# A decoder block on one core: norm weight spread by transposes into PSUM, the first weight tile in token quarters, the compression's transposes two steps later

## The chip, the cores and the metric

One NeuronCore of a Trainium2 chip. The engines are TensorE (PE, with its weight loads as PEld), VectorE (DVE), ScalarE (ACT), GpSimd (POOL) and SyncE (SP), which here issues nearly all DMAs. Times are microseconds of the device for one execution; a result is the median of several runs.

## The reference, cut to what matters

A pre-norm block over 512 tokens of width 1024, in fp32: an RMSNorm, one wide input projection, two attention mixers (A: an indexer picks the top 128 keys; B: 8 heads in 2 groups with a compressed, a selected and a window branch), a gated merge, and a squared-ReLU MLP.

```
h = rmsnorm(x, norm_mix[l])          # x * rsqrt(mean(x*x) + EPS) * norm_mix
proj = h @ w_in[l]
...
blk = blk.transpose(0, 1, 3, 2, 4).reshape(B, n_c, G, CMP_BLOCK * D)
return jax.nn.gelu(blk @ w1) @ w2    # compress_blocks: keys and values of 31 blocks
...
o = (gb[:, :, 0, :, :, None] * o_c + gb[:, :, 1, :, :, None] * o_s
     + gb[:, :, 2, :, :, None] * o_w)
```

## The kernel before

Products are kept near fp32 by splitting each operand into a high part (fp32r) and a remainder: `mm3` adds high x high, high x low and low x high. The high part is a cast on ScalarE, the low part a subtraction (for weights on GpSimd, for activations mostly on VectorE).

**The start.** The 512 tokens come as four tiles x0 to x3 of 128. For each tile `squares(j)` lets ScalarE square it with a row sum and take the root; `scaled(j, half)` lets VectorE multiply 512 columns by the row factor and by `gmix`, the norm weight on all 128 partitions; `turned(j, half)` transposes four 128x128 blocks on TensorE into a PSUM tile `tr` (two buffers), from which ScalarE writes `hTh` and VectorE `hTl`, the normed activations with features on partitions. Three weight tiles of 128 columns (`wf` 0 to 2, made by `split_first`) then give the products `pks`, `pqb0` and `pkw`: `first_tile(i)` yields them one matmul at a time, 24 per half of the tokens (16 with the high weights, 8 with the low ones), and the program hand-places these steps between the transposes (`first_steps`). The order on TensorE, VectorE and ScalarE in this part mostly follows the written one; each engine executes its list strictly in order. `warm_up(n)` puts n idle matmuls on TensorE. Then come `ptok` (the values of all tokens) and the jobs.

**The middle.** Attention runs as 96 small units; per unit TensorE makes logits, VectorE the biased minimum (`nls`, `nlw`), ScalarE the exponential (`pbs`, `pbw`), TensorE transposes (`ts`, `tw`), VectorE and ScalarE write `PTs`, `PTw`, and `ob` multiplies by the values. Between the steps TensorE does projection matmuls (`pqb`, `pg`) from a queue of jobs, and at two places per unit `hook` advances one step of a list of side jobs: `cmp_keys`, `cmp_values` and, per group, `cmp_probs`. `turned_hidden` transposes the hidden layer of the compression (`zk` to `ztk`, `zv` to `ztv`); it waits until `zk` is in the program and then `YH` further steps. If a head ends before its group's compressed probabilities `PTc` are in the program, its compressed product is put into `late[g]` and made at the end of `cmp_probs` (`oc`). TensorE's order in this part is the written one. On the other engines the framework's scheduler orders the instructions.

`split_both` writes the two head pairs of a group as high and low part (`obh`, `obl`) for the branch-B products, which start after head 7.

Of the kernel before, what the change touches and what calls it, by code (L numbers as in the profile page):

```python
# [38 lines left out]
YV, YK, YT = (2,2,3)  # L39
MB = 2  # L40
LA = 1
YH = 4
SG = ()
NWARM = 12
PITCH = 384
PTW = 1664

# [17 lines left out]
def block_kernel(ctx, tc, x, norm_mix, w_in, pe_k, w1_k, w2_k, pe_v, w1_v, w2_v, rel_bias,  # L65
# [109 lines left out]
        xt.append(t)  # L175

    x_in(0)
    gmix = ep.tile([P, DM], F32, name="gmix")
    gm = rows_of(norm_mix)
    ld(gmix[:, 0:S], gm[:, 0:S])  # L180
    ld(ident, c_id)
    x_in(1)
    ld(gmix[:, S:DM], gm[:, S:DM])
    for a, what in enumerate((C_KS, 2, 3, C_QB, C_KW)):
        if what < NT:
            x_in(what)
        else:
            raws.append(raw_cols([(what, P)], f"wr_f{what}"))
# [20 lines left out]

    def scaled(j, half):  # L210
        cs = slice(half * S, (half + 1) * S)
        V.scalar_tensor_tensor(xs[j][:, cs], xt[j][:, cs], rs[j], gmix[:, cs], op0=ALU.mult, op1=ALU.mult)

    def turned(j, half):

# [7 lines left out]

    wf = []

    def split_first(hi_eng=None):
        wf.append(split_w(raws[len(wf)], [P, KT, P], f"wf{len(wf)}", hi_eng))

    def first_tile(i):
        hi, lo = (lambda y: lambda k: wf[i][y][:, k, :])(0), (lambda y: lambda k: wf[i][y][:, k, :])(1)  # L230
        for half in range(2):
            ts = slice(half * 256, half * 256 + 256)
            yield from mm3_steps(outs[i][:, ts], hi, lo, lambda k: hTh[:, k, ts], lambda k: hTl[:, k, ts], KT)

    W = (1,2,2,2)
    squares(0)()
    scaled(0, 0)
    recip1 = squares(1)
    warm_up(W[0])
    l00 = turned(0, 0)  # L240
    scaled(0, 1)
    recip1()
    scaled(1, 0)
    l00()
    warm_up(W[1])
    l01 = turned(0, 1)
    scaled(1, 1)
    split_first()
    l01()
    warm_up(W[2])  # L250
    l10 = turned(1, 0)
    l10()
    recip2 = squares(2)
    warm_up(W[3])
    l11 = turned(1, 1)
    recip2()
    scaled(2, 0)
    l11()
    outs = [ps("mm", "pks"), ps("mm", "pqb0"), None]
    ft = [first_tile(i) for i in range(3)]  # L260

    def first_steps(i, n):
        for _ in range(n):
            next(ft[i])

    SP = (5, 10, 6, 2)
    scaled(2, 1)
    recip3 = squares(3)
    first_steps(0, SP[0])
    l20 = turned(2, 0)  # L270
    recip3()
    scaled(3, 0)
    l20()
    split_first()
    first_steps(0, SP[1])
    l21 = turned(2, 1)
    scaled(3, 1)
    l21()
    first_steps(0, SP[2])
    l30 = turned(3, 0)  # L280
    l30()
    first_steps(0, 24 - SP[0] - SP[1] - SP[2])
    first_steps(1, SP[3])
    l31 = turned(3, 1)
    l31()
    first_steps(1, 24 - SP[3])
    split_first()
    wt_h = ep.tile([P, KT, 352], F32R, name="wt_h")
    wt_l = ep.tile([P, KT, 352], F32R, name="wt_l")
    for k in range(0, KT, 4):  # L290
        A.copy(wt_h[:, k:k + 4], wt_r[:, k:k + 4])
        G.tensor_sub(wt_l[:, k:k + 4], wt_r[:, k:k + 4], wt_h[:, k:k + 4].bitcast(F32))
    outs[2] = ps("lg", "pkw")
    for i in (2, 0, 1, 2):
        first_steps(i, 24)
    for f in ft:
        for _ in f:
            pass
# [555 lines left out]
    def cmp_probs(g):  # L854

        def run():
            cbias = t2.tile([P, NT, 4, 32], F32, tag="cbias", name=f"cbias{g}")
            bt = t2.tile([P, 512], F32, tag="wk", bufs=3, name=f"bt{g}")
            for r in range(4):
                src = d_fwd[:, 4 * g + r]  # L860
                ld(bt[32 * r:32 * r + 32],
                   bass.AP(tensor=src.tensor, offset=src.offset + 496, ap=[[8 * LF - 16, 32], [1, 512]]))
            yield
            yield
            yield
            t = ps("ov", f"cbt{g}")
            for j in range(NT):
                PE.transpose(t[:, j * P:(j + 1) * P], bt[:, j * P:(j + 1) * P], ident)
            yield
            V.tensor_copy(cbias.rearrange("p j h c -> p (j h c)"), t)  # L870
            ptc = t2.tile([P, 2, S], F32R, tag="ptc", bufs=1, name=f"PTc{g}")
            for j in range(0, NT, 2):
                yield
                lg = ps("ov", f"lc{g}{j}")
                for jj in range(2):
                    for r in range(4):
                        c0 = 256 * jj + 64 * r
# [12 lines left out]
                yield  # L890
                A.activation(L, L, AF.Exp)
                yield
                yield
                s = t2.tile([P, 16], F32, tag="cs", bufs=1, name=f"cs{g}{j}")[:, :8]
                V.reduce_sum(s, L, axis=AX.X)
                V.tensor_scalar(s, s, 1.0e-30, None, op0=ALU.max)
                V.reciprocal(s, s)
                V.tensor_mul(s, s, gcmp[:, g, j:j + 2].rearrange("p j r -> p (j r)"))
                V.tensor_tensor(L, L, s[:, :, None].to_broadcast([P, 8, 32]), op=ALU.mult)
                for _ in range(YT):  # L900
                    yield
                t = ps("ov", f"tc{g}{j}")
                for jj in range(2):
                    PE.transpose(t[:, jj * P:(jj + 1) * P],
                                 L[:, 4 * jj:4 * jj + 4].rearrange("p r c -> p (r c)"), ident)
                yield
                js = slice(j * P, (j + 2) * P)
                A.copy(ptc[:, 0, js], t[:, :2 * P])
                V.tensor_sub(ptc[:, 1, js], t[:, :2 * P], ptc[:, 0, js].bitcast(F32))
            PTc[g] = ptc  # L910
            for f in late[g]:
                yield
                rest = f()
                yield
                if rest:
                    rest()

        return run

    late = [[], []]  # L920


    class Unit:
# [109 lines left out]
    def nsa_end(h, PTw, box):  # L1033
        def last():
            o, g = box[0], h // 4
            direct = PTc[g] is not None
            yield from av_steps(o, PTw(), 3 + g, False, not direct)
            if direct:
                cmp_av(o, h, False)
            assert h != 4 or PTc[0] is not None  # L1040
            if h % 2 == 0:
                ob.append(fp.tile([P, S], F32, tag="opb", bufs=2, name=f"opb{h}"))
            aux.append(lambda: add_o(o, ob[h // 2], h % 2, True))
            if not direct:
                def add(pr=ob[-1]):
                    o = ps("ov", f"oc{h}")
                    cmp_av(o, h, True)
                    return lambda: add_o(o, pr, h % 2, False)

                late[g].append(add)  # L1050
            if h % 2 == 1:
                jobs.insert(0, q_job("a", h // 2))
            if h == 3:
                side.append(cmp_probs(1)())
            if h % 4 == 3:
                def split_pair(pr):
                    oh = t1.tile([P, S], F32R, tag=f"kk{g}", bufs=4, name=f"obh{pr}")
                    ol = t1.tile([P, S], F32R, tag=f"kk{g}", bufs=4, name=f"obl{pr}")
                    A.copy(oh, ob[pr])
                    G.tensor_sub(ol, ob[pr], oh.bitcast(F32))  # L1060
                    obp.append((oh, ol))

                def split_both():
                    aux.extend(lambda pr=pr: split_pair(pr) for pr in (h // 2 - 1, h // 2))

                if direct:
                    split_both()
                else:
                    late[g].append(split_both)
            if h == 7:  # L1070
                cps.close()
                op[0] = pool(os_, "op", "left")
                jobs.extend(branch_b_job(c) for c in range(8))
            yield

        return last
# [529 lines left out]
```

## Time and profile before

| | us |
|---|---|
| median of 3 runs | 791.1 (789.76 to 792.16) |
| the profiled execution, its own time | 791.72 |
| its span in the profile | 789.9 |
| TensorE busy | 752.7 (95% of the span) |
| VectorE busy | 578.7 (73%) |
| ScalarE busy | 470.8 (60%) |
| GpSimd busy | 290.4 (37%) |

The span is the profiled execution from its first to its last instruction; its own time lies 1.8 us above it. A row of the profile names the line, the engine, the operation, output and inputs, the count and the time; in brackets stands the idle time of the engine just before and what ended it.

### The profile page before, as it was taken

To read this page: it belongs to the slowest core of one execution; us is meant where nothing else is said; L and a number is where in the kernel's file an instruction comes from. 1 tells how busy PE (TensorE), PEld (TensorE's weight loads), DVE (VectorE), ACT (ScalarE), POOL (GpSimd) and SP (SyncE) were. 2 spreads that over 40 slices of the span, in tenths; PEclk is the share of its full clock that TensorE was granted. 3 is DMA by queue.
4 is the path that set the end of the run, shared out by engine and by line. 5 is a ranking of instruction groups with operands and counts; after the bars stand their busy time and mean duration, and the time that the engine had idled before them with its cause. 6 is when DMAs were issued, how large, how long until landed. Compare 5 with 4: busy or idle time off the path is not lost.

```text
span 789.9 us, 12161 instructions
## 1 busy us (share of the span) xinstructions
PE 752.7 (95%) x4267; PEld 645.9 (82%) x4267; DVE 578.7 (73%) x1301; ACT 470.8 (60%) x975; POOL 290.4 (37%) x183
## 2 busy tenths in 40 slices
PE   7999898999999999989999979999999999999996
PEld 4888687777887788867877979888888999999985
DVE  5344678999999966656747999778778696877444
ACT  6533786778667889985344755645454454644234
POOL 3714643232332347763122862312223141414022
PEclk9999999999999999999999999999999999999999
DMA  9454736253344425464630623222314141413002
GB/s 293 112 165 136 202 88 164 80 141 93 94 140 117 153 69 169 140 229 163 237 107 15 225 81 107 80 89 76 130 54 160 54 160 54 161 54 107 1 27 108
DMA packets 87502, 95.55 MB, mean 121 GB/s; under 512 B 8598, under 2 KB 69654, under 8 KB 87408
## 3 DMA queue, kind: packets, MB, share of 16 engines
q1 hardware_dynamic: 83984, 92.97, 36.9%
q0 software_dynamic: 3456, 1.80, 1.2%
q8 instruction: 34, 0.56, 0.3%
q14 instruction: 28, 0.23, 0.1%
HBM read 86.29 MB, written 14.74 MB: 128 GB/s over the span
## 4 chain that ended last, share of the span: by engine, by line
PE 66%; DVE 19%; ACT 6%; DMA 5%; issue 2%; POOL 1%; SPq 0%; DVEq 0%; ACTq 0%; POOLq 0%
PE mo L1551 8%; PE mo L1554 7%; PE mo L1552 7%; PE z L117 6%; PE z L113 6%; PE z L114 6%; PE wo L1438 2%; PE pg L125 2%; PE pg L123 2%; DVE work L667 2%; PE pg L128 2%; DVE ws L1330 2%; DVE m L666 2%; DVE work L648 1%; DMA w1rv<-in_cmp_w_v 1%
## 5 line engine op out<-in xcount | busy, mean ns | idle before, releaser
L1552 PE MATMUL mo<-wmoh,al 128*128 128x512 f32 (+1 forms) x260 | 100.6, 390 | 0.6 <-DVE al L1494 0.6
L1551 PE MATMUL mo<-wmoh,ah 128*128 128x512 f32 (+1 forms) x260 | 100.9, 393 | 0.3 <-ACT ah L1492 0.2
L1503 POOL TENSOR_TENSOR wmol<-wmor,wmoh 128x1024 fp32r<-128x1024 f32 x17 | 49.6, 2921 | 114.1 <-ACT wmoh L1502 114.0
L1334 POOL TENSOR_TENSOR wm<-wmi,wm 128x512 fp32r<-128x512 f32 x32 | 50.1, 1583 | 109.5 <-ACT wm L1333 109.5
L1333 ACT CAST wm<-ws 128x512 fp32r<-128x512 f32 x80 | 49.3, 622 | 49.4 <-PE z L117 25.3
L1555 DVE SCALAR_TENSOR_TENSOR x<-mo,r,x 128x512 f32<-128x512 f32 (+1 forms) x65 | 47.7, 739 | 41.2 <-PE mo L1554 41.0
L1554 PE MATMUL mo<-wmol,ah 128*128 128x512 f32 (+1 forms) x260 | 70.3, 392 | 0.0
L106 POOL TENSOR_TENSOR wg_l<-wr_g,wg_h 128x1024 fp32r<-128x1024 f32 x16 | 38.4, 2401 | 80.2 <-PE pg L128 29.6
L113 PE MATMUL z<-xshh,wm 128*128 128x256 f32 x256 | 64.1, 283 | 2.5 <-DVE zt L1350 2.5
L1350 DVE TENSOR_TENSOR zt<-zt,z 128x256 f32<-128x256 f32 x128 | 48.6, 413 | 23.4 <-ACT zt L1348 16.8
L114 PE MATMUL z<-xshl,wm 128*128 128x256 f32 x256 | 63.9, 282 | 0.0
L1330 DVE TENSOR_TENSOR ws<-wmi 128x512 f32<-128x512 f32 x74 | 62.3, 852 | 1.0 <-POOL wm L1334 0.7
L1348 ACT ACTIVATE zt<-z 128x256 f32<-128x256 f32 x64 | 22.5, 384 | 65.8 <-PE z L117 65.8
L1551 PEld LDWEIGHTS mo<-wmoh,ah 128*128 128x128 f32 x260 | 48.7, 188 | 11.7 <-DVE x L1555 0.6
L1334 DVE TENSOR_TENSOR wm<-ws,wm 128x512 fp32r<-128x512 f32 x70 | 52.3, 763 | 8.2 <-ACT wm L1333 8.2
L1552 PEld LDWEIGHTS mo<-wmoh,al 128*128 128x128 f32 x260 | 48.9, 188 | 11.2 <-DVE al L1494 0.8
L1554 PEld LDWEIGHTS mo<-wmol,ah 128*128 128x128 f32 x260 | 48.6, 188 | 11.0
L1502 ACT CAST wmoh<-wmor 128x1024 fp32r<-128x1024 f32 x32 | 32.1, 1050 | 41.5 <-PE mo L1552 35.1
L123 PE MATMUL pg<-hTh,wg_h 128*128 128x512 f32 x128 | 53.0, 414 | 0.0
L125 PE MATMUL pg<-hTl,wg_h 128*128 128x512 f32 x128 | 52.6, 411 | 0.0
L113 PEld LDWEIGHTS z<-xshh,wm 128*128 128x128 f32 x256 | 48.7, 190 | 2.9 <-issue 1.7
L114 PEld LDWEIGHTS z<-xshl,wm 128*128 128x128 f32 x256 | 48.7, 190 | 0.0
(427 smaller groups left out, 2206.3 us busy)
## 6 DMA issues: line engine op xcount, KB each, us to landing
wmi<-in_w_mlp_in SPq DMA_DIRECT2D x32, 512.0 KB, 4.8
wmor<-in_w_mlp_out SPq DMA_DIRECT2D x32, 512.0 KB, 3.6
wr_g<-in_w_in SPq DMA_DIRECT2D x16, 512.0 KB, 3.8
d_rev<-d_vr SPq DMA_DIRECT2D x8, 640.0 KB, 5.7
x<-in_x SPq DMA_DIRECT2D x8, 512.0 KB, 7.8
d_t<-th SPq DMA_DIRECT2D x16, 256.0 KB, 2.0
stb<-d_rev SPq DMA_DIRECT2D x8, 256.0 KB, 2.8
wr_qa<-in_w_in SPq DMA_DIRECT2D x4, 512.0 KB, 3.6
```

The costliest lines, as they stand in the source:

```text
L113: PE.matmul(o, wh(k), xh(k), start=start and n == 0, stop=False)
L114: PE.matmul(o, wh(k), xl(k), start=False, stop=False)
L123: PE.matmul(o, wh(k), xh(k), start=k == 0, stop=False)
L125: PE.matmul(o, wh(k), xl(k), start=False, stop=False)
L1330: V.tensor_tensor(t, src, more[0], op=w_blocks[m][2])
L1333: A.copy(w[:, 0], src)
L1334: (V if p > 1 and m in LOV else G).tensor_sub(w[:, 1], src, w[:, 0].bitcast(F32))
L1350: V.tensor_tensor(c, c, o, op=ALU.add if sign > 0 else ALU.subtract)
L1503: (V if ff % 4 in LOO and ff else G).tensor_sub(lo, r, hi.bitcast(F32))
L1551: PE.matmul(o, act[f][0][:, js], wm[f][0][:, cs], start=f == 0, stop=False)
L1552: PE.matmul(o, act[f][1][:, js], wm[f][0][:, cs], start=False, stop=False)
L1554: PE.matmul(o, act[f][0][:, js], wm[f][1][:, cs], start=False, stop=f == FG - 1)
```

## The change

```
-YH = 4
+YH = 6
...
-NWARM = 12
+NWARM = 6
+WU = (2, 1, 1)
...
-    gmix = ep.tile([P, DM], F32, name="gmix")
-    gm = rows_of(norm_mix)
-    ld(gmix[:, 0:S], gm[:, 0:S])
     ld(ident, c_id)
+    g8 = ep.tile([8, P], F32, name="g8")
+    ld(g8, norm_mix.rearrange("(k p) -> k p", p=P))
     x_in(1)
-    ld(gmix[:, S:DM], gm[:, S:DM])
-    for a, what in enumerate((C_KS, 2, 3, C_QB, C_KW)):
+    for what in (C_KS, 2, C_QB, 3, C_KW):
...
-        V.scalar_tensor_tensor(xs[j][:, cs], xt[j][:, cs], rs[j], gmix[:, cs], op0=ALU.mult, op1=ALU.mult)
+        V.scalar_tensor_tensor(xs[j][:, cs], xt[j][:, cs], rs[j], gmix[half], op0=ALU.mult, op1=ALU.mult)
...
+    def split_first():
+        raw, n = raws[len(wf)], len(wf)
...
+        A.copy(hi, raw)
+        for k in range(0, KT, 4):
+            G.tensor_sub(lo[:, k:k + 4], raw[:, k:k + 4], hi[:, k:k + 4].bitcast(F32))
...
+    def norm_rows():
+
+        t = ps("pt", "g_t")
+        PE.transpose(t[:, :8], g8, ident[:8, :8])
+        gT = ep.tile([P, 8], F32, name="gT")
+        V.tensor_copy(gT, t[:, :8])
+        res = [ps("ov", f"gmix{half}") for half in range(2)]
+        for k in range(KT):
+            PE.transpose(res[k // 4][:, k % 4 * P:k % 4 * P + P], gT[:, k:k + 1].to_broadcast([P, P]), ident)
+        return res
...
+    ft = [first_tile(0, ((0, 128), (128, 128), (256, 256)))] + [first_tile(i, ((0, 256), (256, 256))) for i in (1, 2)]
...
     l10 = turned(1, 0)
+    first_steps(0, 8)
     l10()
+    l11 = turned(1, 1)
+    l11()
     recip2 = squares(2)
+    first_steps(0, 16)
+    first_steps(0, 24)
     recip2()
     scaled(2, 0)
+    split_first()
+    l20 = turned(2, 0)
...
+    first_steps(0, 24)
+    first_steps(1, 24)
...
-    for i in (2, 0, 1, 2):
-        first_steps(i, 24)
+    first_steps(2, 48)
...
                 if rest:
                     rest()
+                    yield
+            late_done[g] = True
...
-                if direct:
+                if late_done[g]:
                     split_both()
```

The norm weight is no longer written to 128 partitions by two DMAs: 4 KB are loaded as eight rows, one transpose and a copy turn them into a column per 128 features, and eight transposes of that column, repeated 128 times, leave it on all partitions in two PSUM tiles, which `scaled` reads. The first weight tile's product is made for tokens 0 to 127, 128 to 255 and 256 to 511 instead of two halves; the second tile's first half stands among the transposes of x2 and x3; the second halves of the first two tiles and all of the third follow. Warm-up matmuls go from 19 to 10. The low parts of the three first weight tiles are made in halves. In the middle, the compression's transposes come two steps later, each deferred compressed product takes one more step, and a group's `split_both` waits for the last of them.

SP's list is the order in which the DMAs are issued. Before, its head is:

```order
L174 DMA x_102<-in_x 128x1024
L180 DMA gmix<-in_norm_mix 128x512
L181 DMA ident<-in_c_id 128x128
L174 DMA x_107<-in_x 128x1024
L183 DMA gmix<-in_norm_mix 128x512
L95 DMA wr_f_110<-in_w_in 128x8x128
```

With the change:

```order
L175 DMA x_102<-in_x 128x1024
L179 DMA ident<-in_c_id 128x128
L181 DMA g_105<-in_norm_mix 8x128
L175 DMA x_107<-in_x 128x1024
L96 DMA wr_f_109<-in_w_in 128x8x128
```

x1 (the second `x` row) and everything behind it stand behind 68 KB instead of 320 KB after x0.

TensorE's list at the transposes of the second and third token tile (`tr_0` and `tr_1` are the two halves of a tile) before:

```order
L218 MATMUL tr_1_194<-ident,xs_146 128x128 x4
L123 MATMUL pks<-hTh,wf_h 128x256
L125 MATMUL pks<-hTl,wf_h 128x256
L123 MATMUL pks<-hTh,wf_h 128x256
L125 MATMUL pks<-hTl,wf_h 128x256
L123 MATMUL pks<-hTh,wf_h 128x256
L218 MATMUL tr_0_217<-ident,xs_186 128x128 x4
```

and with the change the last rows of the second token quarter ahead of the third tile's first transposes, where 48 matmuls of 128 columns (8 of them ahead of the second tile's `tr_1`) take the place of those five:

```order
L126 MATMUL pks<-hTl,wf_h 128x128
L124 MATMUL pks<-hTh,wf_h 128x128
L126 MATMUL pks<-hTl,wf_h 128x128
L129 MATMUL pks<-hTh,wf_l 128x128 x8
L217 MATMUL tr_0_263<-ident,xs_210 128x128 x4
L124 MATMUL pqb_132<-hTh,wf_h 128x256
```

TensorE's list at the compression's transpose of the values (`ztv`) before, in the middle of the kernel:

```order
L123 MATMUL pg_1389<-hTh,wg_h 128x512
L934 MATMUL lgs_0_1394<-ksh_404,ub_0_1109 128x128
L935 MATMUL lgs_0_1394<-ksl_405,ub_0_1109 128x128
L779 MATMUL ztv<-ident,zv 128x64
L125 MATMUL pg_1389<-hTl,wg_h 128x512
L123 MATMUL pg_1389<-hTh,wg_h 128x512
```

and with the change, where the rows from `lgs_0` to here hold eleven `pg` matmuls, three transposes `tw_2` and a `sc_0` product:

```order
L126 MATMUL pg_1420<-hTl,wg_h 128x512
L952 MATMUL lgs_1_1467<-ksh_435,ub_0_1137 128x256
L953 MATMUL lgs_1_1467<-ksl_436,ub_0_1137 128x256
L795 MATMUL ztv<-ident,zv 128x64
L124 MATMUL pg_1420<-hTh,wg_h 128x512
```

Ahead of its `ztv`, TensorE now has these to do. The keys' transpose `ztk` moves in the same way, from just ahead of the first head's `ob` products to behind them and behind `lgs_0` of the next head.

## Rows read from the trace of the kernel before

**Rows 1.** The page's head: the span, and the busy time of TensorE and VectorE with its share of the span and the number of instructions.

```profile
span 789.9 us, 12161 instructions
PE 752.7 (95%) x4267; PEld 645.9 (82%) x4267; DVE 578.7 (73%) x1301; ACT 470.8 (60%) x975; POOL 290.4 (37%) x183
```

**Rows 2.** Busy time by stretch of the start: from and to, length, busy time (and instructions) of PE, PEld, DVE, ACT and POOL, then the clock that TensorE was granted (1.00 is 2.4 GHz, 0.50 is 1.2 GHz), the DMA share and GB/s.

```profile
7.36:9.80 2.44, 1.06 (x6) 0.55 (x6) 0.80 (x2) 1.44 (x5) 0.00 (x0) 1.00 1.11 371
9.80:13.26 3.46, 3.46 (x13) 2.25 (x13) 2.80 (x6) 2.65 (x6) 1.09 (x3) 0.51 1.05 392
13.26:16.30 3.04, 1.46 (x10) 1.08 (x9) 2.30 (x4) 2.98 (x7) 2.34 (x1) 1.00 1.20 346
16.30:20.31 4.01, 4.01 (x33) 3.80 (x33) 3.98 (x6) 2.86 (x5) 1.73 (x1) 1.00 1.14 315
20.31:22.16 1.85, 0.00 (x0) 0.00 (x1) 1.85 (x3) 0.03 (x1) 0.64 (x1) 1.00 0.24 29
23.45:26.80 3.35, 3.35 (x17) 3.14 (x15) 0.69 (x1) 3.35 (x3) 2.34 (x1) 0.50 0.98 291
26.80:40.19 13.39, 13.39 (x108) 12.52 (x107) 3.90 (x8) 6.25 (x10) 11.29 (x6) 1.00 0.29 81
```

**Rows 3.** The same columns for the middle, around the compression's two transposes and behind them.

```profile
94.36:98.13 3.77, 0.00 (x1) 0.01 (x1) 3.60 (x8) 3.31 (x10) 1.27 (x1) 1.00 0.08 20
98.13:102.50 4.37, 4.37 (x17) 3.87 (x18) 3.57 (x14) 2.69 (x6) 1.28 (x1) 0.61 0.40 113
125.78:128.31 2.53, 0.00 (x0) 0.00 (x1) 2.50 (x6) 2.07 (x5) 2.08 (x1) 1.00 1.08 355
128.31:132.50 4.19, 4.19 (x14) 3.40 (x15) 4.12 (x19) 1.59 (x4) 0.00 (x0) 0.62 0.47 132
132.50:205.00 72.50, 69.23 (x360) 56.77 (x359) 70.49 (x225) 54.45 (x125) 20.46 (x12) 1.00 0.34 97
```

**Rows 4.** What the DMA engines moved in the first 10 us, in 40 slices of 0.25 us: share of the time busy in tenths, and GB/s.

```profile
DMA  0000000967999997822234794989999999999999
GB/s 0 0 0 0 0 0 0 180 115 311 410 442 360 352 344 197 164 45 64 78 111 51 76 125 160 382 342 442 426 369 393 397 342 350 340 354 348 375 447 401
```

**Rows 5.** ScalarE in order of time: start, length, instruction.

```profile
4.05 1.06 ACT L204 ACTIVATE xs<-x 128x1024 f32<-128x1024 f32 x1 [1.81 <-DMA x<-in_x]
5.24 0.30 ACT L206 ACTIVATE rstd<-ss,small 128x1 f32<-128x1 f32 x1
8.36 1.06 ACT L204 ACTIVATE xs<-x 128x1024 f32<-128x1024 f32 x1 [2.82 <-DMA x<-in_x]
9.54 0.30 ACT L206 ACTIVATE rstd<-ss,small 128x1 f32<-128x1 f32 x1
10.95 0.59 ACT L221 CAST hTh<-tr 128x512 fp32r<-128x512 f32 x1 [0.64 <-PE tr L218]
11.44 1.05 ACT L103 CAST wf_h<-wr_f 128x1024 fp32r<-128x1024 f32 x1
```

**Rows 6.** VectorE in the start.

```profile
6.15 0.75 DVE L212 SCALAR_TENSOR_TENSOR xs<-x,rstd0i,gmix 128x512 f32<-128x512 f32 x1 [0.42 <-DMA gmix<-in_norm_mix]
9.00 0.75 DVE L212 SCALAR_TENSOR_TENSOR xs<-x,rstd0i,gmix 128x512 f32<-128x512 f32 x1 [2.10 <-DMA gmix<-in_norm_mix]
13.28 0.69 DVE L222 TENSOR_TENSOR hTl<-tr,hTh 128x512 fp32r<-128x512 f32 x1 [0.60 <-ACT hTh L221]
18.79 2.71 DVE L212 SCALAR_TENSOR_TENSOR xs<-x,rstd3i,gmix 128x512 f32<-128x512 f32 x1
23.47 0.69 DVE L222 TENSOR_TENSOR hTl<-tr,hTh 128x512 fp32r<-128x512 f32 x1 [0.77 <-ACT hTh L221]
```

**Rows 7.** GpSimd's first two weight subtractions.

```profile
13.21 2.39 POOL L106 TENSOR_TENSOR wf_l<-wr_f,wf_h 128x1024 fp32r<-128x1024 f32 x1
18.58 2.37 POOL L106 TENSOR_TENSOR wf_l<-wr_f,wf_h 128x1024 fp32r<-128x1024 f32 x1 [2.98 <-ACT wf_h L103]
```

**Rows 8.** TensorE: two neighbours of the first products at full clock, a group of four transposes, the last group of them, and eight products of 64 columns with weights of their own.

```profile
17.00 0.28 PE L125 MATMUL pks<-hTl,wf_h 128*128 128x256 f32 x1
17.12 0.28 PE L123 MATMUL pks<-hTh,wf_h 128*128 128x256 f32 x1
19.11 0.60 PE L218 MATMUL tr<-ident,xs 128*128 128x128 f32 x4
22.16 0.66 PE L218 MATMUL tr<-ident,xs 128*128 128x128 f32 x4 [1.85 <-DVE hTl L222]
152.85 0.97 PE L878 MATMUL lc<-KKc,ub 128*128 128x64 f32 x8
```

**Rows 9.** Around the keys' transpose (ScalarE, VectorE, TensorE) and the values' transpose (VectorE, TensorE), in order of time.

```profile
91.18 0.62 ACT L725 CAST w1v<-w1rv 128x512 fp32r<-128x512 f32 x1 [3.61 <-DMA w1rv<-in_cmp_w_v]
97.20 0.69 DVE L971 TENSOR_TENSOR PTs<-ts,PTs 128x512 fp32r<-128x512 f32 x1
98.13 0.27 PE L779 MATMUL ztk<-ident,zk 64*128 64x64 f32 x1 [3.77 <-DVE zk L764]
126.04 1.90 DVE L763 TENSOR_SCALAR uv<-uv 64x128 f32<-64x128 f32 x1
128.31 0.27 PE L779 MATMUL ztv<-ident,zv 64*128 64x64 f32 x1 [2.53 <-DVE zv L764]
```

**Rows 10.** One of the compression's VectorE instructions, by tile: four of them, duration in ns as min, median and max, first and last start.

```profile
L887 DVE TENSOR_SCALAR cm<-cm x4: 150/158/2490, 160.4 to 231.5; 128x8 f32<-128x8 f32 x4
```

More of the change, by code (lines that the diff above doesn't have):

```diff
@@ L224, in block_kernel, with first_tile, first_steps @@
     wf = []
-    def split_first(hi_eng=None):
-        wf.append(split_w(raws[len(wf)], [P, KT, P], f"wf{len(wf)}", hi_eng))
-    def first_tile(i):
+    def split_first():
+        raw, n = raws[len(wf)], len(wf)
+        hi = wp.tile([P, KT, P], F32R, tag="wh", bufs=3, name=f"wf{n}_h")
+        lo = wp.tile([P, KT, P], F32R, tag="wl", bufs=3, name=f"wf{n}_l")
+        A.copy(hi, raw)
+        for k in range(0, KT, 4):
+            G.tensor_sub(lo[:, k:k + 4], raw[:, k:k + 4], hi[:, k:k + 4].bitcast(F32))
+        wf.append((hi, lo))
+    def first_tile(i, parts):
         hi, lo = (lambda y: lambda k: wf[i][y][:, k, :])(0), (lambda y: lambda k: wf[i][y][:, k, :])(1)
-        for half in range(2):
-            ts = slice(half * 256, half * 256 + 256)
+        for t0, n in parts:
+            ts = slice(t0, t0 + n)
             yield from mm3_steps(outs[i][:, ts], hi, lo, lambda k: hTh[:, k, ts], lambda k: hTl[:, k, ts], KT)
-    W = (1,2,2,2)
-    squares(0)()
+    def norm_rows():
[7 more added lines that the diff above has]
+        return res
+    outs = [ps("mm", "pks"), ps("mm", "pqb0"), None]
+    ft = [first_tile(0, ((0, 128), (128, 128), (256, 256)))] + [first_tile(i, ((0, 256), (256, 256))) for i in (1, 2)]
+    def first_steps(i, n):
+        for _ in range(n):
+            next(ft[i])
+    recip0 = squares(0)
+    gmix = norm_rows()
+    recip0()
     scaled(0, 0)
     recip1 = squares(1)
-    warm_up(W[0])
+    scaled(0, 1)
+    warm_up(WU[0])
     l00 = turned(0, 0)
-    scaled(0, 1)
+    split_first()
     recip1()
@@ L244, in block_kernel @@
     l00()
-    warm_up(W[1])
+    warm_up(WU[1])
     l01 = turned(0, 1)
     scaled(1, 1)
-    split_first()
     l01()
-    warm_up(W[2])
+    warm_up(WU[2])
     l10 = turned(1, 0)
+    first_steps(0, 8)
     l10()
+    l11 = turned(1, 1)
+    l11()
     recip2 = squares(2)
-    warm_up(W[3])
-    l11 = turned(1, 1)
+    first_steps(0, 16)
+    first_steps(0, 24)
     recip2()
     scaled(2, 0)
[L258 to L266, printed above, removed]
+    split_first()
+    l20 = turned(2, 0)
     scaled(2, 1)
+    l20()
     recip3 = squares(3)
-    first_steps(0, SP[0])
-    l20 = turned(2, 0)
+    first_steps(1, 8)
+    l21 = turned(2, 1)
     recip3()
     scaled(3, 0)
[L273 to L276, printed above, removed]
+    l21()
+    first_steps(1, 8)
+    l30 = turned(3, 0)
     scaled(3, 1)
-    l21()
-    first_steps(0, SP[2])
-    l30 = turned(3, 0)
     l30()
-    first_steps(0, 24 - SP[0] - SP[1] - SP[2])
-    first_steps(1, SP[3])
+    first_steps(1, 8)
     l31 = turned(3, 1)
     l31()
-    first_steps(1, 24 - SP[3])
     split_first()
+    first_steps(0, 24)
+    first_steps(1, 24)
     wt_h = ep.tile([P, KT, 352], F32R, name="wt_h")
@@ L916, in run @@
                     rest()
+                    yield
+            late_done[g] = True
         return run
-    late = [[], []]
+    late, late_done = [[], []], [False, False]
     class Unit:
```

## The prediction

> **What bounds the kernel now.** The page comes first: TensorE is busy 95% of a span of 789.9 us [rows 1], so a change gains what TensorE loses in waits, at half clock or in work of no use, and only where something else is not full as well. I then cut the time into stretches, read each engine's rows in the start, and last the rows around the two waits of the compression.
>
> The start has three losses [rows 2]. From 7.36 to 9.80 TensorE works 1.06 us of 2.44: the second 512 columns of x0 wait until 9.00 for the second half of `gmix` [rows 6]. From 13.26 to 16.30 it works 1.46 of 3.04. From 20.31 to 22.16 it does nothing: the scaling of x3's second half takes 2.71 us instead of 0.75, because it begins at 18.79 while GpSimd's subtraction runs from 18.58 to 20.95 [rows 6, 7]; the last transposes start at 22.16 [rows 8]. Behind it, from 23.45 to 26.80, the granted clock is 0.50, so 17 matmuls fill 3.35 us [rows 2]. From 26.80 on TensorE is never idle, so a microsecond saved ahead of there moves what follows.
>
> In the middle two waits stand out, 3.77 us before `ztk` and 2.53 us before `ztv` [rows 9], and after each the clock averages 0.61 and 0.62 for some 4 us [rows 3].
>
> **Part 1: the norm weight.** The DMAs show why `gmix` is dear: x0 moves at 300 to 440 GB/s, but from 4.0 to 6.25 us only 45 to 164 GB/s flow, with the first 256 KB of `gmix` in transit [rows 4], which VectorE has at 6.15 [rows 6]. x1 is there only at 8.36 [rows 5]. Without `gmix`, x1's 512 KB follow x0 (there at 4.05) behind 68 KB: at 380 GB/s 1.5 us, so about 5.7. Its square, the small cast and the root took from 8.36 to 9.84 [rows 5]; now they end near 7.2. The weight itself: 4 KB near 4.5, a transpose, a copy, and four transposes at 0.60 [rows 8] give the first half near 6.0, as early as the DMA did, the second near 6.6. So x0's first half is scaled as before, its second at 7.2 to 7.9 instead of 9.00 to 9.75. It can't come earlier: VectorE's list puts ahead of it a small subtraction that waits for ScalarE's cast behind x1's square. From here the second tile's pieces run 2 us ahead.
>
> Reading the weight from PSUM has no row. The nearest is `hTl`, which has one operand in PSUM: 0.69 us, also at 13.28 while GpSimd's subtraction runs [rows 6, 7]. I take 0.75 with no block; if the blocks stayed, x2 and x3 would lose up to 1.96 us (2.71 - 0.75) as now.
>
> **Part 2: the first tile in quarters.** Two quarters need 48 matmuls of 128 columns where one half needed 24 of 256. A 256-column one starts every 0.12 us at full clock [rows 8]. For 128 columns with new weights there is no row; eight of 64 columns take 0.97, or 0.10 each [rows 8]. Between 0.10 and 0.12 I take 0.10, since half the columns should not cost as much as all: 4.8 us instead of 2.9, some 2 us more work, in time where TensorE waited. But the list puts them all ahead of x2's transposes.
>
> Step by step, with 0.75 per scaling, 0.60 per four transposes, 0.59 and 0.69 for `hTh` and `hTl`, 1.05 for a weight cast and 1.5 for square and root [rows 5, 6, 8]: x1's second `hTh` ends near 12.4, its `hTl` near 13.2. The quarters run from 10.2 and end near 15.8, and x2, scaled by 15.0, is transposed only then, to 16.4, half a us before now. x3's square stands behind x2's first `hTh` on ScalarE: root at 18.6, scalings and the `hTl` between them to 21.0, last transposes to 21.7 instead of 22.82.
>
> What then remains on TensorE decides. Before, from 22.82 to 40.19 [rows 2] are 17.37 us: 118 matmuls at 0.12 (14.16), 1.7 lost at half clock (half of 3.35), 1.5 for small products between. After, all of the second weight tile's first half is done: 96 matmuls (11.5), a wait of 0.4 for the last `hTl`, the same 1.5. That gives 21.7 + 13.4 = 35.1 for the same work, 5.1 us ahead, if the clock is full. A second stretch like 23.45 to 26.80 takes 1.7 of it, and I give that even odds, as TensorE has fewer and shorter waits than the 1.85 us ahead of that stretch but also nine warm-ups fewer: 4.2. The other low parts (wt_l and later ones) stay hidden, because GpSimd's list moves up with the casts; uncovered, one costs 2.4 [rows 7]. Part 2's bounds are 1.5 and 5.5.
>
> **Part 3: the compression two steps later.** `ztk` gains almost nothing. Behind it on TensorE stand the `ob` products, and they need `PTs` of the unit, which VectorE writes from 97.20 to 97.89 [rows 9], against 98.13 for `ztk`. Both are late for one reason: ScalarE sat 3.61 us until 91.18 for the DMA of `w1rv` [rows 9], which the change leaves in place. So the wait gets a new name and the clock falls as before: 0.2 us.
>
> `ztv` is another matter on TensorE: eleven `pg` matmuls are now ahead of it, so 2.53 of waiting and 1.6 of lost clock (4.19 x 0.38) [rows 3] can go. But VectorE is busy 2.50 of those 2.53 us, and 70.49 of the 72.5 us that follow [rows 3]. There it sets the pace; TensorE, 4 us ahead, would wait for it later. At most VectorE's own idle 2.0 us can be had, at least nothing: I take 0.8.
>
> The extra step after each `oc` and the later `split_both` cost nothing as long as branch B's products stand far behind them, after head 7; uncovered, its two subtractions are no longer than two of [rows 7], 4.8 us.
>
> **Sum.** 4.2 + 0.2 + 0.8 = 5.2. The profiled execution took 791.72, which gives 786.5; it lies 0.6 above the median of 791.1, so 786 as a median, 0.6% faster.
>
> **The rivals.** *The clock stays low through the start.* At 0.51 from 9.80 to 13.26, TensorE filled 3.46 us with 13 instructions [rows 2]. If the transposes of the weight and both quarters ran at half rate, 1.2 us are lost ahead of x0's transposes and up to 2 more in the quarters: part 2 shrinks to about 1.5, total 789. For it: nine fewer warm-ups, and TensorE idle between the weight's steps. Against it: after 13.26 the clock stayed at 1.00 through a stretch that was only half busy [rows 2].
> The Trainium skill ("TensorE: Matmul & The Clock Gate", "What's actually happening") says that low is the default and that sustained activity lifts it. By that rule this rival would be the likelier one; the trace agrees that the clock falls behind waits, and shows nothing of the new list.
>
> *The lead is swallowed.* The transfers before 91 (`w1rv` and those ahead of it) or VectorE's full stretch could end at the same time whatever the start does. Against it: `w1rv` is issued behind work that TensorE's own progress releases, so it should move along. It would be 791.
>
> *The compression's waits go with their clock.* If `PTs` and `zv` came early enough for TensorE's gain to count, 2.53 + 1.6 and the 1.7 lost behind `ztk` (4.37 x 0.39) add up to 5.8 instead of 1.0: 781. VectorE's 97% speaks against it.
>
> *Slower.* The compression's VectorE instructions fall anew on GpSimd's subtractions. `cm` takes 0.16 us as a rule and 2.49 once, `uv` 1.90 [rows 9, 10]. In VectorE's full stretch each such hit of about 2 us is paid in full. From three hits more than now they eat the start's gain, at four more it is 794. Nothing in the order says they become more; they can as well become fewer.
> The Trainium skill ("SBUF — State Buffer", "Who interferes with whom") has the two engines exclude each other when VectorE reads two SBUF operands or uses two ports; by it the scalings can no longer be hit, the compression's steps can.
>
> **Chances.** Forecast 0.58, larger gain 0.12, low clock 0.13, swallowed 0.10, slower 0.07. A measurement can tell 0.3% (2.4 us) here, so same is 788.7 to 793.5: 0.10 from the swallowed lead, half of the low clock, 0.03 of the forecast. Faster 0.74, same 0.19, slower 0.07. The range 781.5 to 790 leaves out the swallowed lead, the slower case and the far end of the larger gain. The forecast's own is 784 to 788.5.
>
> **What would show it.** Right: x1's square starts near 6, no scaling of x above 0.8 us, the last `hTl` starts about 1 us before 23.47 [rows 6], `ptok` starts 3 to 5 us earlier, no clock of 0.50 between 20 and 35; TensorE still idle near 90 us, now before `ob`; VectorE above 95% through some 70 us behind that. Wrong: x1 still late, 128-column matmuls slower than 0.12, last transposes later than 22, or a lead at `ptok` that is gone at 200.

## The result, and the profile after

The changed kernel takes 785.5 us as a median of 8 runs (780.5 to 792.8), the kernel before 789.1 over its 8 runs beside it. The ratio is 0.9941, with a 95% interval of 0.9913 to 0.9968; a second set of runs (e5 below) gave 0.9960 (0.9939 to 0.9980). So it is faster by 0.4 to 0.6%, and the forecast of 786.0 stands within 0.5 us. Three single executions that stand apart are left out of the ratios: 792.8 here, 913.5 in e3 and 1222.2 in e10.

The sum behind the forecast doesn't stand: it gave the start 4.2 us and the middle 1.0. The traces show 2.8 and 3.2, the timings of each part alone some 1 (e1, e10) and 1.9 (e2). So the close hit is in part luck. A start that was put too high and a middle that was put too low make up for each other, and the forecast was taken off 791.1, while before gave 789.1 beside the change: 5.2 us were forecast, and measured are 3.6 by the medians and 4.7 by the ratio.

The profiled execution of the changed kernel took 782.65, 2.9 below its median, that of before 791.72, 2.6 above its own. The two traces therefore lie 9.0 us apart, and the kernels some 4. A single pair of traces can't be differenced here, so every part below is read from several.

The page's head (as [rows 1]):

```profile
span 780.9 us, 12210 instructions
PE 749.2 (96%) x4291; PEld 645.0 (83%) x4291; DVE 576.5 (74%) x1302; ACT 469.2 (60%) x975; POOL 291.0 (37%) x186
```

The start by stretch (columns as in [rows 2]: length, busy time of PE, PEld, DVE, ACT and POOL, granted clock, DMA share, GB/s):

```profile
9.80:10.93 1.13, 0.54 (x5) 0.16 (x3) 1.13 (x3) 0.95 (x2) 0.88 (x2) 1.00 1.09 413
10.93:14.30 3.37, 3.37 (x17) 3.37 (x18) 1.89 (x3) 0.59 (x1) 2.65 (x3) 0.51 1.13 315
14.30:18.77 4.47, 4.47 (x42) 4.47 (x41) 2.26 (x4) 2.87 (x5) 1.28 (x2) 0.98 1.19 257
18.77:22.52 3.75, 2.96 (x27) 2.79 (x26) 1.75 (x4) 2.40 (x5) 1.23 (x1) 1.00 0.24 41
24.57:37.20 12.63, 12.63 (x103) 12.03 (x102) 5.16 (x9) 10.60 (x14) 11.02 (x5) 1.00 0.36 104
```

The clock is at half from 10.93 to 14.30, and TensorE then goes through both quarters without a gap; the 3.35 us at half clock behind the last transposes [rows 2] have no counterpart.

The first 10 us of the DMAs (as [rows 4]), x1's square on ScalarE (as [rows 5]), and x3's second scaling on VectorE (as [rows 6]):

```profile
GB/s 0 0 0 0 0 0 0 180 197 262 360 344 360 358 300 199 217 262 329 279 327 259 305 327 319 360 342 367 426 369 442 414 352 365 360 330 375 340 402 426
7.31 1.06 ACT L203 ACTIVATE xs<-x 128x1024 f32<-128x1024 f32 x1 [1.63 <-DMA x<-in_x]
22.89 0.74 DVE L211 SCALAR_TENSOR_TENSOR xs<-x,rstd3i,gmix 128x512 f32<-128x512 f32 x1
```

x1 is there at 7.31 instead of 8.36, and no scaling takes above 0.75.

The middle on TensorE, at the attention products that [rows 9] has just behind `ztk`, and at `ztk` itself:

```profile
92.51 0.51 PE L1009 MATMUL ob<-PTs,VV 128*128 128x512 f32 x1 [0.61 <-ACT PTs L988]
94.53 0.98 PE L1009 MATMUL ob<-PTs,VV 128*128 128x512 f32 x4 [1.52 <-DVE PTs L989]
96.87 0.27 PE L795 MATMUL ztk<-ident,zk 64*128 64x64 f32 x1
```

The 3.77 us in one piece have become 0.61 and 1.52, for `PTs` as forecast, and the granted clock behind them is 1.00 up to 130. `ztv` waits for nothing.

### The profile page after: what moved, and what is told of

It reads as the page before. It is cut to its first block, busy times and chain, and to the rows that moved or that the text cites. A ratio compares the mean times of both kernels' runs of the same rounds, so it can differ in the third digit from the quotient of the medians.

```text
span 780.9 us, 12210 instructions
## 1 busy us (share of the span) xinstructions
PE 749.2 (96%) x4291; PEld 645.0 (83%) x4291; DVE 576.5 (74%) x1302; ACT 469.2 (60%) x975; POOL 291.0 (37%) x186
## 4 chain that ended last, share of the span: by engine, by line
PE 71%; DVE 18%; ACT 4%; DMA 4%; issue 2%; POOL 0%; SPq 0%; DVEq 0%; ACTq 0%; POOLq 0%
PE mo L1569 8%; PE mo L1572 8%; PE mo L1570 7%; PE z L118 6%; PE z L114 6%; PE z L115 6%; PE wo L1456 2%; DVE work L683 2%; PE pg L129 2%; PE pg L126 2%; PE pg L124 2%; DVE m L682 2%; DVE ws L1348 2%; PE ob L1009 1%; PE oa L1009 1%
## 5 line engine op out<-in xcount | busy, mean ns | idle before, releaser
L1351 ACT CAST wm<-ws 128x512 fp32r<-128x512 f32 x80 | 49.1, 620 | 49.3 <-PE z L118 27.1
L1348 DVE TENSOR_TENSOR ws<-wmi 128x512 f32<-128x512 f32 x74 | 64.0, 872 | 2.2 <-DMA wmi<-in_w_mlp_in 1.3
L1352 DVE TENSOR_TENSOR wm<-ws,wm 128x512 fp32r<-128x512 f32 x70 | 50.3, 735 | 7.7 <-ACT wm L1351 7.7
```

The lines of the kernel that those rows point to most:

```text
L1348: V.tensor_tensor(t, src, more[0], op=w_blocks[m][2])
L1351: A.copy(w[:, 0], src)
L1352: (V if p > 1 and m in LOV else G).tensor_sub(w[:, 1], src, w[:, 0].bitcast(F32))
```

## The experiments

Each ratio is against the kernel before, on the same chip.

| kernel | median us | ratio | 95% interval |
|---|---|---|---|
| e1, start alone | 786.9 | 0.9986 | 0.9962 to 1.0011 |
| e10, start alone again | 786.9 | 0.9989 | 0.9960 to 1.0018 |
| e2, middle alone | 786.7 | 0.9976 | 0.9959 to 0.9993 |
| e7, `YH` alone | 787.7 | 0.9996 | 0.9978 to 1.0014 |
| e3, weight alone | 787.7 | 0.9998 | 0.9977 to 1.0019 |
| e4, all but the weight | 789.3 | 1.0007 | 0.9984 to 1.0031 |
| e5, whole change again | 784.5 | 0.9960 | 0.9939 to 0.9980 |
| e9, whole, two steps | 792.1 | 1.0052 | 1.0023 to 1.0081 |
| e6, whole, `w1rv` earlier | 782.2 | 0.9936 | 0.9909 to 0.9962 |
| e12, the same again | 781.3 | 0.9932 | 0.9902 to 0.9962 |

e8 and e11 were run once each (784.6 and 829.7) and have no ratio; they are read for their traces.

Two measures come from each trace. The first is the start of the first side product (`pkc`) on TensorE, behind all of the start. The second is the time from the first `pki` to the first `lga`, a stretch that holds the same work in each kernel. It is cut at the first `h1v`, the values' first product of the compression, which stands behind `ztk` and ahead of `ztv`. "Half clock" (1.2 of 2.4 GHz) is the time lost to it by the records: one minus the granted clock, summed over slices of 1 us.

| trace | start | half clock ahead of 55 us | `pkc` |
|---|---|---|---|
| before | old | 1.7 at 9-14, 1.7 at 23-27 | 56.8 |
| e7 | old | 1.7 at 12-16 | 56.2 |
| e2 | old | none | 55.3 |
| e3 | weight | 1.7 at 7-12 | 53.9 |
| e8 | weight | none | 53.2 |
| after, e10 | new | 1.7 at 11-15 | 54.4, 54.4 |
| e1, e5, e9 | new | none | 52.3, 52.6, 52.6 |
| e6, e12 | new | none | 52.3, 53.0 |

The records don't show all of it. In the five traces of the last two rows the weight's eight transposes near 5 us take 1.97 us, against 1.09 in after and e10, at a recorded clock of 1.00. Little hangs on it here, as x0's second half is scaled only at 8.1 us or later.

| trace | steps | idle ahead of `ztk` or `ob` | ahead of `ztv` | half clock | `pki` to `h1v` | `h1v` to `lga` | `pki` to `lga` |
|---|---|---|---|---|---|---|---|
| before | 4 | 3.8 | 2.5 | 3.4 | 28.6 | 172.1 | 200.7 |
| e1 | 4 | 2.1 | 2.5 | 3.4 | 26.9 | 172.1 | 199.0 |
| e10 | 4 | 2.6 | 2.5 | 1.7 | 25.8 | 172.1 | 197.9 |
| e3 | 4 | 3.8 | 2.5 | 3.4 | 29.0 | 172.0 | 201.0 |
| e8 | 4 | 2.3 | 2.5 | 1.7 | 25.4 | 172.1 | 197.5 |
| after | 6 | 2.1 | 0 | 0 | 25.8 | 170.6 | 196.4 |
| e5 | 6 | 1.7 | 0 | 0 | 25.4 | 170.6 | 196.0 |
| e2 | 6 | 1.9 | 0 | 1.7 | 27.0 | 170.0 | 197.0 |
| e7 | 6 | 1.1 | 0 | 0 | 24.5 | 171.0 | 195.5 |
| e4 | 6 | 1.3 | 0 | 0 | 24.6 | 170.7 | 195.3 |
| e9 | 2 | 5.4 | 3.0 | 6.8 | 31.3 | 173.2 | 204.5 |

### e1 and e10: the start alone

```
-YH = 6
+YH = 4
...
-                    yield
-            late_done[g] = True
...
-                if late_done[g]:
+                if direct:
```

> Only the start is changed (weight by transposes, quarters, new order, ten warm-ups); the compression's transposes stay 4 steps behind and the split of a group is as before. Theory A (the prediction's: the start gives nearly all of it): the first side products start 2.4 us earlier as in the whole change, that lead is still there at the end, 0.35 to 0.5% faster. The keys' transpose still waits in one piece, 2.5 to 3.8 us, and the clock falls behind it. Theory B (the later transposes give more than half): the lead stays at 2.4 us or less up to the end, 0.2 to 0.3% faster, and the lead of 5 us that the whole change has at 105 us is missing. Rival C (the lead is lost to later waits): within 0.15% of before.

> The start alone once more, for its size. Theory A (start and middle add to the whole's 0.4%): 0.15 to 0.3% faster. Rival B (the lead of the start is lost again in the waits near 95 and 125 us, with their stretches at half clock): within 0.1% of before.

In the traces `pkc` comes at 52.3 and 54.4 us. Ahead of it the two executions differ in a stretch at half clock. Both keep the wait ahead of `ztv`, and `pki` to `lga` is no longer than in before (199.0 and 197.9 beside 200.7), so the traces show no later wait that takes the lead back. The timings show 0.14 and 0.11%, with intervals from a gain of 0.4% to a loss of 0.2%. By size that is e1's rival C and e10's rival B, though not by their mechanism; the smaller gain of e1's theory B and e10's theory A lie inside the intervals, so none is settled.

### e2 and e7: the middle alone, and the number alone

e2 is the kernel before with the three edits of the middle; e7 with this only:

```
-YH = 4
+YH = 6
```

> Only the middle is changed: transposes of the compression 6 steps behind instead of 4, one more step for each deferred product, the split waits for the deferred ones. Theory A: no lead up to 94 us, TensorE idle 3 to 3.8 us ahead of the attention products near 95 us and the clock low behind, lead after the values' transpose at most 1 us, 0.1% faster. Theory B: the idle time at 95 us breaks into two pieces below 2.5 us in all or the clock stays full, and a lead of 2.5 us or more stands at the values' first product (110.6 us before), 0.35 to 0.7% faster.

> The kernel before with one number changed: the compression's transposes 6 steps behind instead of 4; the split and the deferred products as before. Theory A (the later transposes are all of the middle's gain): 0.2 to 0.3% faster as with the three edits of the middle together, no wait ahead of the values' transpose. Rival B (the split that waits, or the further step, gives or costs something): more than 0.15% away from those three together.

Theory B holds in e2's trace: the wait broken in two, no wait ahead of `ztv`, the values' first product 3.1 us earlier (1.5 of them from the start, which had no half clock this time). Its size doesn't: 0.24% faster, where 0.35 to 0.7 were expected. e7 shows the same in its trace, and even the shortest middle with the old start, but its timing shows no gain. The intervals of the two overlap, and e7's profiled execution lost 3.4 us at half clock at 333 to 340. By size (0.04% against 0.24%) that is e7's rival B; whether the split that waits, or the further step, gives anything is not settled.

### e3 and e8: the weight alone

Before's order of the start, with `norm_rows` and the DMA of 4 KB in place of the two DMAs of `gmix`.

> Only the norm weight is changed: spread by transposes into two PSUM tiles; halves, order of the start, 19 warm-ups and the middle as before. Theory A (reading the weight from PSUM ends the block by GpSimd, and x1 comes earlier): x1's square near 7.3 us, the scaling of x3's second half 0.75 us although GpSimd's subtraction of 2.4 us runs beside it, last transposes 1.5 to 2.5 us earlier than 22.16, 0.2 to 0.35% faster. Rival B (x and the output in SBUF are enough for the block): that scaling still takes above 2 us, last transposes less than 1 us earlier, 0.1% faster or less. Rival C: the weight's own transposes at half clock delay x0's, and nothing is left at 40 us.

> The kernel with only the norm weight changed, a second look at its start. Theory A (stretches at half clock in the first 25 us are chance, and the weight alone gives the start's gain): no stretch at half clock between 8 and 11 us this time, or another place for it; at full clock the first side products at 52 to 53 us, as in the start alone. Rival B (the kernel itself brings the half clock there, by the weight's transposes): the same stretch from 8 to 10.8 us again, and 53.9 us.

e3 holds the direct test of the block. VectorE and GpSimd in e3:

```profile
19.32 0.74 DVE L210 SCALAR_TENSOR_TENSOR xs<-x,rstd3i,gmix 128x512 f32<-128x512 f32 x1
19.11 2.39 POOL L106 TENSOR_TENSOR wf_l<-wr_f,wf_h 128x1024 fp32r<-128x1024 f32 x1 [2.19 <-ACT wf_h L103]
```

The scaling lies wholly inside GpSimd's subtraction, as in [rows 6, 7], and takes 0.74 instead of 2.71; only the weight's place has changed. Theory A of e3 holds on that, while its forecast of the time doesn't: 0.9998. In e8 no stretch at half clock shows and `pkc` comes at 53.2, close to its theory A (52 to 53). By these single traces without a recorded stretch, the weight alone gives 55.3 - 53.2 = 2.1 us, and the new order 0.6 to 0.9 more.

### e4 and e11: everything but the weight

```
-    g8 = ep.tile([8, P], F32, name="g8")
-    ld(g8, norm_mix.rearrange("(k p) -> k p", p=P))
...
+    ld(gmix[:, 0:S], gm[:, 0:S])
...
-    gmix = norm_rows()
```

> The whole change except the weight, which comes by the two DMAs into SBUF as before (the weight's transposes are gone too, and with them eight early matmuls). Theory A (quarters and order are only worth it behind an early x1): x1's square at 8.4 us, quarters end 1 to 2 us later than 18.8 us, the first side products 0 to 1 us earlier than before instead of 2.4, so 1.4 to 2.4 us are lost against the whole change (0.2 to 0.3%). Rival B (the order alone gives the start's gain): the first side products start 2 us or more earlier than before, 0.5 to 0.6% faster as the whole change. On the block: GpSimd's subtractions in halves are 1.2 us each; a scaling that falls on one takes 1.2 us or more if the weight in SBUF is what lets it be blocked, 0.75 otherwise.

> The whole change without the weight's transposes (the weight by two DMAs), a second look at its start, where TensorE ran 128-column products at 0.18 us each from 11 to 25 us. Theory A (chance): at full speed this time, first side products at 53.5 to 55 us. Rival B (ten warm-ups without the eight transposes of the weight leave TensorE slow in this order): the same slow stretch of more than 6 us, first side products behind 57 us.

In both, TensorE is slow from about 11 to 25 us. e4, two neighbours of the quarters, and e11 by stretch:

```profile
20.33 0.41 PE L124 MATMUL pks<-hTh,wf_h 128*128 128x128 f32 x1
20.54 0.41 PE L126 MATMUL pks<-hTl,wf_h 128*128 128x128 f32 x1
```

```profile
8.00:10.00 2.00, 0.67 (x5) 0.27 (x3) 1.00 (x4) 1.72 (x5) 0.00 (x0) 0.58 1.14 377
11.50:25.00 13.50, 13.50 (x65) 13.50 (x66) 4.18 (x8) 4.57 (x9) 6.32 (x5) 0.50 0.97 270
```

One of 128 columns starts every 0.21 us in e4, though its records grant a clock of 1.00 there, and e11's records give 0.50 for the same. `pkc` comes at 59.5 and 61.2, so in e4 2.7 us later than in before, where both of its theories had it earlier. Both traces have the slow stretch and none of the seven others with this order, so e11's rival B is far likelier than chance: the rival "the clock stays low through the start" is what happens here. Why isn't shown. TensorE's idle time doesn't tell these traces apart: from 6 to 10 us it works for 2.1 us in e4, 1.2 in e11 and 1.9 in after. (e11's granted clock stayed at 0.85 to its end, so only its start is read.)

On the block, no scaling begins inside a subtraction in e4 or e11. It is the other way round: x2's second scaling is under way when GpSimd's subtraction begins, keeps its 0.75, and the subtraction's two halves take 2.99 in both traces. With the weight in PSUM the same overlap costs nothing (GpSimd in e4, then in after):

```profile
17.68 2.99 POOL L233 TENSOR_TENSOR wf_l<-wr_f,wf_h 128x512 fp32r<-128x512 f32 x2 [3.08 <-ACT wf_h L231]
17.49 2.52 POOL L231 TENSOR_TENSOR wf_l<-wr_f,wf_h 128x512 fp32r<-128x512 f32 x2 [3.91 <-ACT wf_h L229]
```

So with both operands in SBUF it was the engine that began later that lost the time, VectorE in [rows 6, 7] and GpSimd here.

### e5: the whole change again

> The whole change once more, beside the same runs of before as the next two, and a second trace of it. Theory A (the parts add: start and middle each some 2 to 3 us): 0.4 to 0.6% faster; in the trace no wait ahead of the values' transpose, less than 2.5 us idle ahead of the first attention products, and first side products at 52.5 to 54.5 us, by whether a stretch at half clock falls into the first 25 us. Rival B (the parts overlap, as both shorten the same wait near 95 us): 0.25 to 0.35% faster.

0.40% faster, 0.20 to 0.61: nearer to theory A, without excluding B. Its start has no recorded half clock, with `pkc` at 52.6.

### e9: two steps instead of six

```
-YH = 6
+YH = 2
```

> The whole change with the compression's transposes 2 steps behind instead of 6. Theory A (TensorE's waits for zk and zv cost what they last, and VectorE doesn't take it back): ahead of each of the two transposes 4 to 5 us of idle time in one piece (what the start alone showed, 2.1 and 2.5, and some ten products of 0.23 us that now stand behind), each with a low clock behind; 0.5 to 0.9% slower than the whole change. Rival B (the prediction's: VectorE sets the pace behind the values' transpose): the wait before zv is longer, but 0.25% slower at most.

TensorE's two waits in e9, and then the stretch from the first `pki` to the first `lga` in before, after and e9:

```profile
92.50 0.36 PE L795 MATMUL ztk<-ident,zk 64*128 64x64 f32 x1 [5.36 <-DVE zk L780]
125.06 0.27 PE L795 MATMUL ztv<-ident,zv 64*128 64x64 f32 x1 [2.97 <-DVE zv L780]
```

```profile
82.00:282.70 200.70, 187.73 (x980) 155.57 (x979) 182.94 (x590) 149.41 (x346) 68.34 (x44) 0.98 0.43 122
```

```profile
79.60:276.00 196.40, 185.76 (x981) 153.21 (x979) 183.04 (x590) 148.70 (x346) 68.24 (x44) 1.00 0.43 125
```

```profile
77.80:282.30 204.50, 189.43 (x980) 157.67 (x979) 182.33 (x590) 149.60 (x346) 68.54 (x44) 0.97 0.43 120
```

It is 0.52% slower than before and 0.9% slower than the whole change (1.0052 / 0.9960), as theory A has it. The wait at `ztk` grew more than expected and that at `ztv` less. Of the 8.1 us that `pki` to `lga` takes longer than in after, 5.5 lie ahead of `h1v` and 2.6 behind it. Rival B spoke of the wait before `zv` alone: those 2.6 us are 0.33%, with two stretches at half clock of 1.7 in them, one behind `ztv` and one near 200 us. So the total speaks against it, and the part that it is about does so less. VectorE is busy for 182.3 to 183.0 us in all three; what varies is its own idle time, 17.8, 13.4 and 22.2 us. So over the whole of this stretch it isn't full.

### e6 and e12: w1rv one gate tile earlier

```
-    JO = "kc vc qi0 qi1 hk0 hk1 ki qb1 g0 hv0 hv1 qb2 g1 qb3".split()
+    JO = "kc vc qi0 qi1 hk0 hk1 ki qb1 hv0 hv1 g0 qb2 g1 qb3".split()
```

> The whole change, and the first half of the values' compression weight (w1rv) is loaded and cast one gate tile earlier (jobs in the order qb1, hv0, hv1, g0 instead of qb1, g0, hv0, hv1). Theory A (ScalarE's wait for w1rv near 88 us is the cause of TensorE's idle time ahead of the attention products): ScalarE waits less than 0.5 us for w1rv, TensorE's 2.1 us of idle time there shrink below 0.7, 0.2 to 0.3% faster than the whole change. Rival B (the wait is passed on, to the gate tile's weights or to the second half): the idle time stays near 2 us under another name and the time is that of the whole change within 0.15%.

> The whole change with w1rv one gate tile earlier, once more, for its size against before and for its clock. Theory A (it saves the idle time ahead of the attention products for good): 0.55 to 0.75% faster than before, and where no stretch at half clock falls behind the new waits near 97 and 100 us, a first key block product (lga) 195 us or less behind the first pki. Rival B (the gain of the first timing was chance, the new waits take back what is saved): 0.35 to 0.5% faster, as the whole change.

ScalarE's casts of `w1rv` in e6, and TensorE's waits from 60 to 220 us (in total, times, longest):

```profile
76.81 0.64 ACT L741 CAST w1v<-w1rv 128x512 fp32r<-128x512 f32 x1
84.47 0.62 ACT L741 CAST w1v<-w1rv 128x512 fp32r<-128x512 f32 x1 [1.56 <-DMA w1rv<-in_cmp_w_v]
```

```profile
PE tc L920 <- DVE cl L915: 2.6, 1, 2.6
PE tw L981 <- DVE hsk L814: 1.6, 1, 1.6
PE pg L124 <- DVE ub L345: 1.2, 1, 1.2
PE ob L1009 <- DVE PTs L989: 0.4, 1, 0.4
```

The first half now waits for nothing, its second half for 1.56 us, and `ob` waits 0.4 (0.7 in e12) instead of 2.1. The cause named in the prediction is thereby shown: move `w1rv`, and the wait for `PTs` goes. New waits stand elsewhere, and up to `lga` 5.1 us are lost at half clock in e6 and 1.7 in e12; the stretch takes 196.5 and 194.7 us. Both timings, 0.9936 and 0.9932, are the fastest of all. That this beats the whole change is likely and not proved, as the intervals of e6 and e5 overlap.

## Why the prediction was right, and where it wasn't

**Part 1 was right in kind, its steps late.** x1's square starts at 7.31 (6.72 in e1, 7.08 in e5), forecast 5.7. The step that failed is that x1 would have the DMAs to itself at 380 GB/s. Behind x0 they give 199 to 329 GB/s for some 2.5 us, and from 4.18 to 7.29 they move 1.01 MB, where x1 and the 68 KB ahead of it are 0.59: transfers issued behind x1 moved alongside it. x0's second half is scaled from 8.68 to 9.41, forecast 7.2 to 7.9. That reading the weight from PSUM ends the block is shown by e3. The Trainium skill ("SBUF — State Buffer", "Who interferes with whom") has VectorE free of GpSimd as long as it reads at most one operand from SBUF and doesn't use two ports, and the pair in e3 agrees, 0.74 beside 2.39.

**Part 2's order went as listed, with a larger cost.** A 128-column product starts every 0.11 us at full clock, forecast 0.10:

```profile
14.97 0.27 PE L124 MATMUL pks<-hTh,wf_h 128*128 128x128 f32 x1
15.08 0.28 PE L126 MATMUL pks<-hTl,wf_h 128*128 128x128 f32 x1
```

48 of them are 5.3 us, not 4.8; they end at 18.77, forecast 15.8, with 1.7 us of that from the half clock. The last transposes end at 24.5 instead of 21.7; that item, named as what would show the forecast wrong, did fail. Even without the recorded half clock they end at 22.5 and 22.7 (e1, e5). `ptok` starts 3.0 us earlier, at the low end of the forecast's 3 to 5, but before has done two of its products by then; the lead at `pkc` is 2.4 us in this trace, where 4.2 were forecast for the start.

**The failing step of the start is the clock.** I took two stretches at half clock [rows 2] for a property of before's order. e2, with the same start, has none and reaches `pkc` 1.5 us sooner; e7 has one, elsewhere. Without a recorded stretch the change gives 55.3 to 52.5, some 2.8 us, where the sum gave 5.1, of which 1.7 were that chance stretch. The "even odds" for a stretch in the new order came to 2 of 7 traces in the table above, at 11 to 15 us; behind the transposes none had one.

**The rival with the low clock was near.** In the change itself the start shows only stretches of it, but it is what e4 and e11 show as soon as the weight comes by DMA again. The sum gave the weight's transposes no credit for that; whether they are what spares the change from it is not shown.

**`ztk`: the cause right, the size wrong.** TensorE does wait for `PTs` instead, and `w1rv` is behind it (e6, e12). But `pki` to `h1v` takes 27.1 us on average with 4 steps and 25.4 with 6, 1.7 less, where 0.2 was forecast. The part of the term that failed is "the clock falls as before": half clock followed in three of five traces with 4 steps and in one of five with 6. In the traces where it didn't, the averages are 25.6 and 25.1, so without it the change is worth some 0.5. The first `ob` products need only ScalarE's part of `PTs`, so the wait falls in two. Whether a wait in two pieces brings half clock less often, five traces against five don't show. That `w1rv` comes 1.0 us sooner behind `pki` than in before (2.62 us of waiting instead of 3.61) is chance: e3 and e8, one program, wait 4.00 and 2.01.

**`ztv`: the mechanism held, the term was small.** From `h1v` on, all five traces with 4 steps take 172.0 to 172.1 us to `lga`, and those with 6 steps 170.0 to 171.0, on average 1.5 less, where the sum took 0.8 between 0 and 2.0. What left is the wait of 2.5 us and the 1.7 us of half clock that stood behind it in every one of the five, 4.2 together; so 2.7 came back. As forecast, much of that is waiting for VectorE: after has waits that before doesn't have, for the index selection and the minimum on VectorE:

```profile
PE sc L669 <- DVE work L664: 2.0, 2, 1.4
PE sc L669 <- DVE nms L959: 1.3, 1, 1.3
```

The stretch behind `ztv` [rows 3] holds VectorE as busy after as before:

```profile
128.00:200.00 72.00, 68.62 (x356) 56.29 (x356) 70.91 (x233) 53.65 (x124) 20.98 (x13) 1.00 0.35 98
```

The size is missed because I looked for VectorE's slack in the 72.5 us alone. Over all of `h1v` to `lga` it was idle for 9.1 us, and 1.7 of these are gone (before, then after, columns as in [rows 2]):

```profile
110.60:282.70 172.10, 162.90 (x861) 135.20 (x860) 163.03 (x527) 127.91 (x297) 56.25 (x34) 0.99 0.41 119
105.40:276.00 170.60, 162.09 (x862) 134.02 (x860) 163.21 (x527) 127.32 (x297) 56.16 (x34) 1.00 0.41 120
```

Both parts together: `pki` to `lga` averages 199.2 us over five traces with 4 steps and 196.0 with 6, 3.2 us, where 1.0 was forecast. By mean, idle and half clock at the three places were 8.1 us and are now 2.0; 6.1 removed less the 3.3 of waits for VectorE leaves 2.8, about what the lengths show.

**The other rivals.** The lead was not swallowed before 91, `pki` keeps the 2.4 us of `pkc`. The collisions with GpSimd became no more: VectorE's busy time from `pki` to `lga` is 182.9 and 183.0 us. "The waits go with their clock", given 5.8 us and a chance of 0.12, was right about the clock, behind `ztv` above all. By size the middle's 3.2 us in the traces lie about halfway between it and the forecast's 1.0, and the 1.9 of e2's timing nearer to the forecast.

**What stays open.** The start's lead of some 3 us in the traces is about 1 us in the timings of e1 and e10, whose intervals just reach 3. Both profiled executions are 1.9 us faster than the medians of their kernels, so a part lies in executions that were not traced. The mean granted clock of each run says more of the whole: taken off one and times the span, it gives on average 3.9 us of half clock in e5 and 6.9 in before beside it, a difference of 3.0 where the medians lie 3.6 apart. In e1 and e10 it is 6.3 and 6.6 beside 6.5 and 6.3, in e2 5.5 beside 6.5, in e9 10.5 beside 6.3. So most of what the timings show of the whole change is half clock that is gone, which the start alone doesn't bring; where the rest of the start's lead goes was not found.

## What to carry to other kernels

A stretch at half clock in one trace isn't a term of a sum until a second execution shows it in the same place: the one behind `ztv` was there in every trace with the wait, those of the start were not. An engine that is full behind a wait takes back a part of what the wait gives, not all of it; cut the time at an instruction behind the wait and compare several traces, as 172.1 and 170.6 here. And when work is moved past a wait, ask which operand the next instruction needs first, because the new wait can fall in two pieces.

## What the runs showed of the hardware

**Half clock, in part without a fixed place.** By the records each trace loses 2.6 to 8.7 us of its span to stretches at half clock (130 in e11, left out), most of them 1.7 us each. Behind the wait of 2.5 to 3.0 us ahead of `ztv` one followed in all six traces that have the wait. Near `ztk` one followed in four of the six with a wait of 2.1 to 5.4 us in one piece, and in e2 behind pieces of 0.4 and 1.5. Those near 10 and 335 us come in some executions of one program and not in others. Runs of one program spread by some 1%, which is of the same size.

**Half clock under full load.** In e4 and e11 TensorE was never idle from 11.5 to 25.0 us and still ran at half rate; the products of 256 columns, from 23.6 and 23.9 on, still started every 0.21 us up to 27.0 and 25.4, then every 0.12 to 0.13. In after the same 128-column products began at half clock, from 11.64, and ran at full clock from 14.53. The Trainium skill ("TensorE: Matmul & The Clock Gate", "What's actually happening") has sustained activity lift the clock; after agrees, e4 and e11 don't. What keeps it down was not tested.

**The record of the clock can miss it.** e4's records grant 1.00 through those 13.5 us, and so do those of e1, e5, e6, e9 and e12 while the weight's transposes run at about half pace (1.97 us instead of 1.09). The time from one product to the next shows it.
